# Two transformer blocks on one core: an expert list of 64-byte entries, and the gates' transfers issued by GpSimd in eight pieces

## The chip, the cores and the metric

The kernel is one program on one NeuronCore of a Trainium2 chip. Its engines have their own instruction queues: TensorE (PE; its weight loads are PEld), VectorE (DVE), ScalarE (ACT), GpSimd (POOL) and SyncE (SP). SP, ACT and POOL also issue DMA transfers, which run on 16 DMA engines that the queues share. The metric is the device time of one execution in microseconds (us), lower is better.

## The reference, cut to what matters

Two blocks follow each other on 256 tokens of width 2048. The change lies in the last stage of the second block, a layer that looks up experts. For each token and each of 8 heads it picks 16 of 16,384 experts, and adds up what they give:

```python
sc, ci = lax.top_k(cand, PEER_TOPK)          # cand: sums of two top-16 lists, 256 candidates
idx = e1 * PEER_NKEYS + e2                   # 128 * 128 experts
gate = jax.nn.softmax(sc, axis=-1)
h = jax.nn.gelu(jnp.einsum('cd,chkd->chk', xc, u[ic]))
return jnp.einsum('chk,chkd->cd', gc * h, v[ic])
```

With 256 tokens, 8 heads and 16 picks, most experts are wanted by some token of the 256. The kernel therefore computes `x @ u.T` for all of them, and uses the list of picked experts only for the second product.

## The kernel before, in words

The last stage is the method `peer`. A **group** g (0 to 31) is 512 experts: `fm_group` loads four 1 MB tiles of `in_pu` (SP's queue, L271, three buffers named `raw`), splits each in two halves into a rounded part (ScalarE, L294) and a remainder (VectorE, L295), and multiplies both with the tokens on TensorE (L312 to L314, three matmuls for each product). ScalarE applies GELU (L1526, two rows for each group) into a tile `ge` with two buffers, and GpSimd writes `ge` to rows of the array `R` in device memory (L1528). Each of the four tiles of a group is a **unit**.

Work on the list lies beside the groups. `unit` takes functions from a list `bg` before each load, 1.92 of them for each unit from group 6 on. Those are in order:

- 128 calls of `gates(b, q)`: sixteen of them are a **block** b (0 to 7) of 32 tokens. Each makes one-hot masks on ScalarE (L1412, L1413) and VectorE (L1415), two matmuls (L1417) and an addition into the tile `GB` (two buffers with the tag `gb`). After the sixteenth, the block goes out to `R` and `RD`: L1423 has 15,872 rows of 128 bytes, L1424 has 512 such rows. Both are issued on ScalarE's queue.
- `classes`, `across`, `within`, `places`: each of 15,872 experts gets its place in a list that is sorted by which half of the tokens wants it.
- 31 calls of `scatter` with four indirect transfers each (L1499): each writes 128 expert numbers, 4 bytes each, to their places in `LIST` in device memory.
- `fetch`: when all 124 are complete, the list is read back into `L` (L1506, GpSimd's queue).

After group 31 comes the last part: GpSimd gathers rows of `R` (L1566) and of the experts' values (L1574) by the numbers in `L`, and TensorE multiplies them.

The framework's scheduler fixes the order of each engine's rows before the run. GpSimd's transfers use eight semaphores in turn, so each one also waits until the eighth before it has landed.

Of the kernel before, what the change touches and what calls it, by code (L numbers as in the profile page):

```python
# [11 lines left out]
I32 = mybir.dt.int32  # L12
U32 = mybir.dt.uint32
# [6 lines left out]
P = 128  # L20
T = 256
# [9 lines left out]
EC = 124  # L31
# [96 lines left out]
def prep(i):  # L128
    f = np.float32
    out = {}  # L130
# [5 lines left out]
    o = np.cumsum([0, 256, 256, 512, 512, 16, 1536, 512, 4, 4, 512, 512, 512, 512, 4])  # L136
# [42 lines left out]
    out["pv"] = np.concatenate([pv[:EC].transpose(1, 0, 2).reshape(P * EC, D), pv[EC:].reshape(-1, D)], axis=0)  # L179
    out["ids"] = np.arange(P * EC, dtype=np.int32).reshape(P, EC)  # L180
    out["rel"] = np.concatenate([i["rel_bias_2"], np.ones((1, 32), f)], axis=0)
# [18 lines left out]
class Model:  # L200
# [1149 lines left out]
    def peer(self):  # L1350
# [8 lines left out]
        nc.gpsimd.dma_start(sub, A["subk"].rearrange("p (a n) -> p a n", a=2))  # L1359
        ids = self.t(sp, [P, EC], I32)  # L1360
        nc.gpsimd.dma_start(ids, A["ids"])

        R = self.t(self.dp, [P * EC, 2 * T])
        RD = self.t(self.dp, [P, P - EC, T])
        R3 = R.rearrange("(p e) t -> p e t", p=P)
        LIST = self.t(self.dp, [P * EC, 1], I32)
        E1 = self.t(sp, [P, 2, 8, 16])
# [34 lines left out]
        def gates(b, q):  # L1402
# [19 lines left out]
            if q == 15:  # L1422
                nc.scalar.dma_start(R3[:, :, T + 32 * b:T + 32 * b + 32], GB[0][:, 0:EC])  # L1423
                nc.scalar.dma_start(RD[:, :, 32 * b:32 * b + 32], GB[0][:, EC:P])  # L1424

                dst = F[:, b // 4] if b % 4 == 0 else F4
                nc.vector.tensor_reduce(dst, GB[0], AX.X, ALU.add)
                if b % 4:
                    nc.vector.tensor_add(F[:, b // 4], F[:, b // 4], F4)
# [6 lines left out]
        place, bad = self.t(sp, [P, EC], U32), self.t(ep, [P, 1], I32)  # L1436
        L = self.t(ep, [P, EC], U32)
        got = {}
# [56 lines left out]
        wrote = []  # L1495

        def scatter(lo, hi):
            for e in range(lo, hi):
                i = nc.gpsimd.indirect_dma_start(LIST, bass.IndirectOffsetOnAxis(ap=place[:, e:e + 1], axis=0),  # L1499
                                                 ids[:, e:e + 1], None)  # L1500
                tc.declare_no_dep(i.ins, group="places", reason="the places are different")
                tc.add_to_no_dep_group("places", i.ins)
                wrote.append(i.ins)

        def fetch():
            i = nc.gpsimd.dma_start(L.bitcast(I32), LIST.rearrange("(r c) o -> r (c o)", r=P))  # L1506
            for w in wrote:
                tc.add_manual_dep(i.ins, w.name, mybir.DependencyInfo(mybir.DependencyClass.Sync, mybir.DependencyReason.DATA),
                                  reason="the list is complete")
# [3 lines left out]
        for g in range(32):  # L1513
            if g < 4:
                scores(g)
            if g == 6:
                self.bg.append(turn)
                self.bg += [lambda b=b, q=q: gates(b, q) for b in range(8) for q in range(16)]
                self.bg += [classes, lambda: None, across, lambda: None, within, places]
                self.bg += [lambda e=e: scatter(e, e + 4) for e in range(0, EC, 4)]  # L1520
                self.bg += [fetch]
                self.rate = 1.92
# [39 lines left out]
        def gather(pool, cs):  # L1562

            rt = self.t(pool, [P, 4, 2 * T], tag="rt")
            for e, c in enumerate(cs):
                nc.gpsimd.indirect_dma_start(rt[:, e], None, R, bass.IndirectOffsetOnAxis(ap=L[:, c:c + 1], axis=0))  # L1566
            n = len(cs)
# [5 lines left out]
        def listed(c, r):  # L1573
            nc.gpsimd.indirect_dma_start(r, None, A["pv"], bass.IndirectOffsetOnAxis(ap=L[:, c:c + 1], axis=0))  # L1574
            return r
# [145 lines left out]
```

## Time and profile before

| what | value |
|---|---|
| median of 3 runs | 3310.65 us (3301.16 to 3317.48) |
| the profiled execution's own time | 3312.3 us |
| its span, first to last instruction | 3310.5 us |
| TensorE busy | 2990.0 us (90%) |
| VectorE, ScalarE, GpSimd busy | 2154.5, 1558.8, 498.5 us |
| mean granted TensorE clock | 0.952 of full |
| groups 0 to 31 of the last stage | 1754 to 2804 us of the span |

The profile is of one execution. Issuing a transfer doesn't count as busy time on ScalarE and SP. A busy TensorE says little by itself, so what ends its idle time is read from the waits and from rows in order of time.

### The profile page before, as it was taken

Reading aid. Unit: us, or ns where it says so; the run is one execution under the profiler, and the core shown is the slowest. Engines: PE = TensorE matmul, PEld = TensorE weight load, DVE = VectorE, ACT = ScalarE, POOL = GpSimd, SP = SyncE. Lnnn points to the kernel's source line nnn. Section 1 sums busy time; section 2 is a strip of 40 time slices with the busy share of each in tenths; the row PEclk is TensorE's granted clock in tenths of the full one; section 3 lists DMA queues with packets and bytes.
Section 4 is the critical chain, followed back from the end, with each engine's and each line's share of the span. In section 5 each row is a group of like instructions: output and inputs, shape, how many; then the busy total and the mean of one; then the engine's idle time right before and its main releaser. Section 6 shows DMA issues by size and latency. Waiting matters only on the chain.

```text
span 3310.5 us, 53445 instructions
## 1 busy us (share of the span) xinstructions
PE 2990.0 (90%) x21356; PEld 2781.8 (84%) x21356; DVE 2154.5 (65%) x3842; ACT 1558.8 (47%) x2604; POOL 498.5 (15%) x468
## 2 busy tenths in 40 slices
PE   5989988999999999999999998788883599999998
PEld 4678878999999999887899998788783589777776
DVE  7678987786555555745669977677770134666665
ACT  1163443544444344557554466566550133555545
POOL 3100000000000000200000000000007521556552
PEclk9999999999999999989999999899986799999999
DMA  9955677685655555433345556666661246788886
GB/s 403 386 208 191 216 265 250 218 324 198 245 194 186 183 187 184 163 141 112 129 164 181 183 204 187 177 196 193 181 192 53 96 173 222 263 290 282 299 283 214
DMA packets 253043, 696.66 MB, mean 210 GB/s; under 512 B 149226, under 2 KB 149290, under 8 KB 190832
## 3 DMA queue, kind: packets, MB, share of 16 engines
q1 hardware_dynamic: 75600, 472.29, 40.2%
q0 software_dynamic: 44816, 199.83, 16.8%
q10 hardware_dynamic: 132368, 21.03, 3.6%
q8 instruction: 170, 2.79, 0.3%
q14 instruction: 89, 0.73, 0.1%
HBM read 657.58 MB, written 41.53 MB: 211 GB/s over the span
## 4 chain that ended last, share of the span: by engine, by line
PE 60%; DMA 9%; DVE 8%; issue 7%; ACT 5%; POOL 4%; ACTq 4%; another core or an unknown queue 1%; DVEq 0%; SPq 0%; POOLq 0%
PE t L314 18%; PE t L312 18%; PE t L313 18%; DMA t<-in_wmod 4%; DMA t<-in_pv,t 4%; ACTq L1424 3%; DVE t L295 3%; POOL t L1566 2%; ACT t L294 1%; PE t L310 1%; DVE t L421 1%; PE t L1229 1%; POOL t L1574 1%; ACT t L1260 1%
## 5 line engine op out<-in xcount | busy, mean ns | idle before, releaser
L312 PE MATMUL t<-t,t 128*128 128x256 f32 (+2 forms) x6376 | 1912.8, 301 | 128.6 <-ACT t L294 48.2
L314 PE MATMUL t<-t,t 128*128 128x256 f32 (+2 forms) x6376 | 1905.7, 300 | 42.9 <-DVE t L295 23.8
L313 PE MATMUL t<-t,t 128*128 128x256 f32 (+2 forms) x6376 | 1909.5, 300 | 36.3 <-issue 19.4
L295 DVE TENSOR_TENSOR t<-t,t 128x1024 fp32r<-128x1024 f32 (+2 forms) x938 | 1135.2, 1217 | 808.4 <-ACT t L294 730.0
L294 ACT ACTIVATE t<-t 128x1024 fp32r<-128x1024 f32 (+2 forms) x938 | 982.0, 1052 | 1182.0 <-PE t L313 694.3
L312 PEld LDWEIGHTS t<-t,t 128*128 128x128 f32 x6376 | 1239.3, 194 | 178.6 <-ACT t L294 56.5
L313 PEld LDWEIGHTS t<-t,t 128*128 128x128 f32 x6376 | 1239.8, 194 | 81.4 <-issue 25.7
L314 PEld LDWEIGHTS t<-t,t 128*128 128x128 f32 x6376 | 1237.3, 195 | 83.9 <-DVE t L295 30.2
L421 DVE CUSTOM_DVE_ANT_0 t<-t,t,t 128x1024 f32<-128x1024 f32 x192 | 244.7, 1279 | 59.0 <-DMA t<-in_wmod 58.7
L1415 DVE TENSOR_SCALAR t<-t,t,t 128x128 fp32r<-128x128 f32 x512 | 142.8, 341 | 39.2 <-PE t L1417 39.1
L1574 POOL DMA_INDIRECT t<-in_pv,t x103 | 140.3, 1362 | 179.2 <-DVE t L295 148.1
L1528 POOL DMA_DIRECT2D t<-t x31 | 23.6, 761 | 875.5 <-ACT t L1526 418.5
L1566 POOL DMA_INDIRECT t<-t,t x103 | 137.9, 1339 | 50.7 <-issue 26.8
L1499 POOL DMA_INDIRECT t<-t,t x124 | 126.2, 1018 | 48.0 <-issue 37.5
L310 PE MATMUL t<-t,t 128*128 128x256 f32 (+1 forms) x448 | 116.2, 422 | 13.2 <-ACT t L523 7.1
L310 PEld LDWEIGHTS t<-t,t 128*128 128x128 f32 x448 | 87.5, 197 | 41.8 <-issue 19.7
L1420 ACT ACTIVATE t<-t 128x256 f32<-128x256 f32 x128 | 44.6, 399 | 107.3 <-issue 104.2
L1412 ACT ACTIVATE t<-t,t 128x128 f32<-128x128 f32 x256 | 89.3, 397 | 0.1
L1421 DVE TENSOR_TENSOR t<-t,t 128x256 f32<-128x256 f32 x128 | 49.0, 420 | 60.3 <-ACT t L1420 60.2
L1102 POOL DMA_DIRECT2D t<-in_w2c x1 | 0.6, 564 | 455.3 <-DMA t<-in_win 455.3
L1072 POOL DMA_DIRECT2D t<-in_oh x1 | 0.6, 566 | 454.4 <-PE t L389 454.4
L1417 PE MATMUL t<-t,t 128*128 128x256 f32 x256 | 45.9, 292 | 24.9 <-ACT t L1413 24.8
(393 smaller groups left out, 1821.3 us busy)
## 6 DMA issues: line engine op xcount, KB each, us to landing
t<-in_pu SPq DMA_DIRECT2D x128, 1024.0 KB, 4.8
t<-in_win SPq DMA_DIRECT2D x64, 1024.0 KB, 5.9
t<-in_wmod SPq DMA_DIRECT2D x122, 512.0 KB, 5.9
t<-in_wg SPq DMA_DIRECT2D x44, 1024.0 KB, 4.8
t<-in_wu SPq DMA_DIRECT2D x44, 1024.0 KB, 4.8
t<-in_wd SPq DMA_DIRECT2D x44, 1024.0 KB, 5.0
t<-in_wmod POOLq DMA_DIRECT2D x70, 512.0 KB
t<-in_wout SPq DMA_DIRECT2D x32, 1024.0 KB, 5.4
```

Source lines behind the costliest of these rows:

```text
L294: nc.scalar.activation(h[:, :w], r[:, o:o + w], AF.Copy)
L295: nc.vector.tensor_sub(l[:, :w], r[:, o:o + w], h[:, :w].bitcast(F32))
L310: mm(ps, wh, xh, start=start, stop=stop, skip_group_check=True)
L312: mm(ps, wh, xh, start=start, stop=False, skip_group_check=True)
L313: mm(ps, wh, xl, start=False, stop=False, skip_group_check=True)
L314: mm(ps, wl, xh, start=False, stop=stop, skip_group_check=True)
L421: nc.vector.tensor_tensor_reduce(r, r, self.cb[:, s], 1.0, init, ALU.mult, ALU.add, dst)
L1415: nc.vector.tensor_scalar(o1[:, k], iota, ET[:, 0, t:t + 1], GH[:, k, t:t + 1].bitcast(F32), ALU.is_equal, ALU.mult)
L1424: nc.scalar.dma_start(RD[:, :, 32 * b:32 * b + 32], GB[0][:, EC:P])
L1499: i = nc.gpsimd.indirect_dma_start(LIST, bass.IndirectOffsetOnAxis(ap=place[:, e:e + 1], axis=0), ids[:, e:e + 1], None)
L1566: nc.gpsimd.indirect_dma_start(rt[:, e], None, R, bass.IndirectOffsetOnAxis(ap=L[:, c:c + 1], axis=0))
L1574: nc.gpsimd.indirect_dma_start(r, None, A["pv"], bass.IndirectOffsetOnAxis(ap=L[:, c:c + 1], axis=0))
```

## The change

Part one is the list. An entry of `LIST` grows from one number of 4 bytes to 16 copies of it, 64 bytes; the input `ids` holds each number 16 times, and each scatter writes 128 entries of 64 bytes. `ids` (1 MB in place of 62 KB) is loaded late, by the new `numbers`, into a buffer of the tag `gb`. The fetch (1 MB in place of 62 KB) moves from GpSimd's queue to SP's, and the gathers read every sixteenth number of `L16`. Part two is the gates: the transfer to `R` is issued by GpSimd in eight pieces of 16 partitions (1,984 rows of 128 bytes each), and the one to `RD` by GpSimd behind them.

```diff
@@ -177,7 +177,7 @@
 
     pv = i["peer_v_2"][0].reshape(P, P, D)
     out["pv"] = np.concatenate([pv[:EC].transpose(1, 0, 2).reshape(P * EC, D), pv[EC:].reshape(-1, D)], axis=0)
-    out["ids"] = np.arange(P * EC, dtype=np.int32).reshape(P, EC)
+    out["ids"] = np.repeat(np.arange(P * EC, dtype=np.int32), 16).reshape(P, EC * 16)
     out["rel"] = np.concatenate([i["rel_bias_2"], np.ones((1, 32), f)], axis=0)
     pos = np.concatenate([np.concatenate([i[n][0].T] * 2, axis=0) for n in ("cmp_pos_k_2", "cmp_pos_v_2")], axis=1)
     v = {
@@ -1357,13 +1357,11 @@
         XH, XL = self.XH, self.XL
         sub = self.t(sp, [P, 2, P])
         nc.gpsimd.dma_start(sub, A["subk"].rearrange("p (a n) -> p a n", a=2))
-        ids = self.t(sp, [P, EC], I32)
-        nc.gpsimd.dma_start(ids, A["ids"])
 
         R = self.t(self.dp, [P * EC, 2 * T])
         RD = self.t(self.dp, [P, P - EC, T])
         R3 = R.rearrange("(p e) t -> p e t", p=P)
-        LIST = self.t(self.dp, [P * EC, 1], I32)
+        LIST = self.t(self.dp, [P * EC, 16], I32)
         E1 = self.t(sp, [P, 2, 8, 16])
         E2 = self.t(sp, [P, 2, 8, 16])
         GG = self.t(sp, [P, 2, 8, 16])
@@ -1420,8 +1418,9 @@
             nc.scalar.activation(gb, pv[:, 1], AF.Copy)
             nc.vector.tensor_add(gb, pv[:, 0], gb)
             if q == 15:
-                nc.scalar.dma_start(R3[:, :, T + 32 * b:T + 32 * b + 32], GB[0][:, 0:EC])
-                nc.scalar.dma_start(RD[:, :, 32 * b:32 * b + 32], GB[0][:, EC:P])
+                for p in range(0, P, 16):
+                    nc.gpsimd.dma_start(R3[p:p + 16, :, T + 32 * b:T + 32 * b + 32], GB[0][p:p + 16, 0:EC])
+                nc.gpsimd.dma_start(RD[:, :, 32 * b:32 * b + 32], GB[0][:, EC:P])
 
                 dst = F[:, b // 4] if b % 4 == 0 else F4
                 nc.vector.tensor_reduce(dst, GB[0], AX.X, ALU.add)
@@ -1434,7 +1433,7 @@
         MT, BT = self.t(sp, [EC, 4, P]), self.t(sp, [P, 8])
         PO, PI, PF = self.t(sp, [P, EC]), self.t(sp, [P, 2, EC], I32), self.t(sp, [P, 2, EC])
         place, bad = self.t(sp, [P, EC], U32), self.t(ep, [P, 1], I32)
-        L = self.t(ep, [P, EC], U32)
+        L16 = self.t(ep, [P, EC * 16], U32)
         got = {}
 
         def classes():
@@ -1494,16 +1493,21 @@
 
         wrote = []
 
+        def numbers():
+            got["ids"] = self.t(sp, [P, EC * 16], I32, tag="gb", bufs=2)
+            nc.gpsimd.dma_start(got["ids"], A["ids"])
+
         def scatter(lo, hi):
+            ids = got["ids"]
             for e in range(lo, hi):
                 i = nc.gpsimd.indirect_dma_start(LIST, bass.IndirectOffsetOnAxis(ap=place[:, e:e + 1], axis=0),
-                                                 ids[:, e:e + 1], None)
+                                                 ids[:, 16 * e:16 * e + 16], None)
                 tc.declare_no_dep(i.ins, group="places", reason="the places are different")
                 tc.add_to_no_dep_group("places", i.ins)
                 wrote.append(i.ins)
 
         def fetch():
-            i = nc.gpsimd.dma_start(L.bitcast(I32), LIST.rearrange("(r c) o -> r (c o)", r=P))
+            i = nc.sync.dma_start(L16.bitcast(I32), LIST.rearrange("(r c) o -> r (c o)", r=P))
             for w in wrote:
                 tc.add_manual_dep(i.ins, w.name, mybir.DependencyInfo(mybir.DependencyClass.Sync, mybir.DependencyReason.DATA),
                                   reason="the list is complete")
@@ -1516,7 +1520,7 @@
             if g == 6:
                 self.bg.append(turn)
                 self.bg += [lambda b=b, q=q: gates(b, q) for b in range(8) for q in range(16)]
-                self.bg += [classes, lambda: None, across, lambda: None, within, places]
+                self.bg += [classes, numbers, across, lambda: None, within, places]
                 self.bg += [lambda e=e: scatter(e, e + 4) for e in range(0, EC, 4)]
                 self.bg += [fetch]
                 self.rate = 1.92
@@ -1563,7 +1567,7 @@
 
             rt = self.t(pool, [P, 4, 2 * T], tag="rt")
             for e, c in enumerate(cs):
-                nc.gpsimd.indirect_dma_start(rt[:, e], None, R, bass.IndirectOffsetOnAxis(ap=L[:, c:c + 1], axis=0))
+                nc.gpsimd.indirect_dma_start(rt[:, e], None, R, bass.IndirectOffsetOnAxis(ap=L16[:, 16 * c:16 * c + 1], axis=0))
             n = len(cs)
             WH, WL = weighted(pool)
             nc.vector.tensor_mul(rt[:, :n, 0:T], rt[:, :n, 0:T], rt[:, :n, T:2 * T])
@@ -1571,7 +1575,7 @@
             return WH, WL
 
         def listed(c, r):
-            nc.gpsimd.indirect_dma_start(r, None, A["pv"], bass.IndirectOffsetOnAxis(ap=L[:, c:c + 1], axis=0))
+            nc.gpsimd.indirect_dma_start(r, None, A["pv"], bass.IndirectOffsetOnAxis(ap=L16[:, 16 * c:16 * c + 1], axis=0))
             return r
```

On ScalarE the end of block 1, before the change (`t_20938` is this block's `GB`):

```order
L1412 ACTIVATE t_21745<-t_74,t_16977 128x128
L1412 ACTIVATE t_21753<-t_74,t_16977 128x128
L1423 DMA t_16971<-t_20938 15872x1x32
L1424 DMA t_16972<-t_20938 512x1x32
L1420 ACTIVATE t_21723<-t_21724 128x128x2
L1413 ACTIVATE t_21744<-t_21745 128x128
L1413 ACTIVATE t_21752<-t_21753 128x128
L294 ACTIVATE t_21768<-t_21762 128x1024
L1420 ACTIVATE t_21723<-t_21743 128x128x2
```

The same place after the change (`t_20943` is this block's `GB`; lines are two lower):

```order
L1418 ACTIVATE t_20943<-t_21628 128x128x2
L1418 ACTIVATE t_20943<-t_21647 128x128x2
L1411 ACTIVATE t_21737<-t_21738 128x128
L1411 ACTIVATE t_21745<-t_21746 128x128
L1410 ACTIVATE t_21757<-t_74,t_16975 128x128
L1410 ACTIVATE t_21765<-t_74,t_16975 128x128
L1411 ACTIVATE t_21756<-t_21757 128x128
L1411 ACTIVATE t_21764<-t_21765 128x128
L294 ACTIVATE t_21780<-t_21774 128x1024
```

The two transfers are gone from ScalarE; the next block's masks follow at once on the block's last copies.

On GpSimd, from the write of group 22 to the fetch, before the change (`t_16971` is `R`, `t_16973` is `LIST`, and "x25" is 25 such rows in a run):

```order
L1528 DMA t_16971<-t_26613 128x4x256
L1499 DMA t_16973<-t_16969,t_16989 15872x1 x25
L1528 DMA t_16971<-t_26902 128x4x256
L1499 DMA t_16973<-t_16969,t_16989 15872x1 x43
L1528 DMA t_16971<-t_27172 128x4x256
L1499 DMA t_16973<-t_16969,t_16989 15872x1 x42
L1528 DMA t_16971<-t_27442 128x4x256
L1499 DMA t_16973<-t_16969,t_16989 15872x1 x14
L1506 DMA t_16991<-t_16973 128x124
L1528 DMA t_16971<-t_27708 128x4x256
```

On GpSimd after the change, from the pieces of block 7 to the last scatter (`t_16969` is `R`, `t_16970` is `RD`, `t_16971` is `LIST`, `t_26609` is `ids`; L1532 writes groups 22 to 26 in this order):

```order
L1422 DMA t_16969<-t_25810 1984x1x32 x8
L1423 DMA t_16970<-t_25810 512x1x32
L1498 DMA t_26609<-in_ids 128x1984
L1532 DMA t_16969<-t_26669 128x4x256
L1532 DMA t_16969<-t_26958 128x4x256
L1503 DMA t_16971<-t_26609,t_16987 15872x16 x44
L1532 DMA t_16969<-t_27228 128x4x256
L1503 DMA t_16971<-t_26609,t_16987 15872x16 x32
L1532 DMA t_16969<-t_27498 128x4x256
L1503 DMA t_16971<-t_26609,t_16987 15872x16 x28
L1532 DMA t_16969<-t_27764 128x4x256
L1503 DMA t_16971<-t_26609,t_16987 15872x16 x20
```

The gates' nine transfers and the load of `ids` now stand ahead of the write of group 22, the writes of groups 22 and 23 ahead of the first scatter, and the writes of groups 24, 25 and 26 behind 44, 76 and 104 scatters (before, 23, 24 and 25 behind 25, 68 and 110). The fetch has left this queue.

On SP after the change, around the fetch (L1510):

```order
L271 DMA t_28145<-in_pu 128x2048
L271 DMA t_28203<-in_pu 128x2048
L1510 DMA t_16989<-t_16971 128x1984
L271 DMA t_28267<-in_pu 128x2048
L271 DMA t_28325<-in_pu 128x2048
```

The row of the fetch is new here. The two loads above it are the last of group 28. Below it stand the twelve of groups 29 to 31, of which two are shown.

## Rows read from the trace of the kernel before

**Rows 1.** The page: the span, and two lines of the 40 equal slices (82.8 us each): TensorE's busy tenths and the tenths of full clock that it was granted; then the issues of the groups' loads (count, KB each, median us from issue to landing).
```profile
span 3310.5 us, 53445 instructions
PE   5989988999999999999999998788883599999998
PEclk9999999999999999989999999899986799999999
...
t<-in_pu SPq DMA_DIRECT2D x128, 1024.0 KB, 4.8
```

**Rows 2.** Lines L1423 and L1424 alone (`ACTq` is ScalarE's queue; shortest, median and longest in ns, first and last start in us). The landing time is that of L1423, from issue to the last byte.
```profile
L1423 ACTq DMA_DIRECT2D t<-t x8: 520/521/596, 2003.1 to 2447.5; - x8
DMA to landing us min/median/max: 16.7/16.7/16.7
...
L1424 ACTq DMA_DIRECT2D t<-t x8: 13702/13966/14959, 2003.7 to 2448.1; - x8
```

**Rows 3.** ScalarE in order of time (start us, us): the second of the two GELU rows of groups 7, 8, 9 and 22.
```profile
2001.19 0.58 ACT L1526 ACTIVATE t<-t 128x512 f32<-128x512 f32 x1
2038.73 0.58 ACT L1526 ACTIVATE t<-t 128x512 f32<-128x512 f32 x1
2063.55 0.58 ACT L1526 ACTIVATE t<-t 128x512 f32<-128x512 f32 x1
2468.87 0.60 ACT L1526 ACTIVATE t<-t 128x512 f32<-128x512 f32 x1 [0.46 <-PE t L314]
```

**Rows 4.** Busy time in three stretches, whose columns are: length, busy us of PE, PEld, DVE, ACT, POOL (instructions in brackets), granted clock, busy share of the 16 DMA engines, GB/s. The first stretch is the first gate block before its transfers, the second a hold of ScalarE's queue at L1424, the third the block after it.
```profile
1950.00:2003.00 53.00, 52.89 (x443) 52.72 (x442) 44.82 (x106) 43.31 (x116) 2.26 (x3) 1.00 0.54 192
2323.50:2337.50 14.00, 7.14 (x58) 6.72 (x56) 7.22 (x10) 0.00 (x0) 0.00 (x0) 0.92 1.00 172
2337.50:2385.50 48.00, 46.67 (x363) 46.26 (x364) 39.12 (x87) 38.47 (x100) 1.51 (x2) 0.92 0.56 194
```

**Rows 5.** DMA queues from 2448 to 2466 us, which holds one block's transfers: packets, MB, share of the 16 engines (q10 is ScalarE's queue, q1 SP's).
```profile
q10 hardware_dynamic: 16416, 2.10, 74.3%
q1 hardware_dynamic: 34, 0.16, 5.3%
```

**Rows 6.** What a plain DMA costs GpSimd: L419 (128 rows of 4 KB, 537 ns in the mean, from the groups by line), L1528 (512 rows of 1 KB, shortest, median, longest), the two L1082 in order of time (2048 rows of 1536 bytes each; in square brackets the idle time before and what ended it), and the landing of the last L1528 out of the chain of work (start us, us).
```profile
L419 POOL DMA_DIRECT2D t<-in_wmod x70 | 37.4, 537 | 88.0 <-DMA t<-in_wmod 52.6 <-DVE t L421 15.8 <-DVE t L541 6.1
L1528 POOL DMA_DIRECT2D t<-t x31: 754/754/806, 1757.0 to 2778.5; - x31
874.67 1.04 POOL L1082 DMA_DIRECT2D t<-t  x1 [2.53 <-DMA t<-t]
895.66 1.03 POOL L1082 DMA_DIRECT2D t<-t  x1 [19.45 <-DMA t<-t]
2778.53 3.66 DMA t<-t
```

**Rows 7.** GpSimd: the scatters as a whole, then rows in order of time from the first scatter to the fetch (square brackets: the idle time before, and what ended it).
```profile
L1499 POOL DMA_INDIRECT t<-t,t x124: 967/971/1883, 2482.0 to 2675.2; - x124
2481.96 1.07 POOL L1499 DMA_INDIRECT t<-t,t  x1 [10.54 <-DVE t L1484]
2515.50 0.81 POOL L1528 DMA_DIRECT2D t<-t  x1
2570.54 0.97 POOL L1499 DMA_INDIRECT t<-t,t  x1 [0.30 <-issue]
2593.13 0.81 POOL L1528 DMA_DIRECT2D t<-t  x1 [21.62 <-ACT t L1526]
2678.04 0.58 POOL L1506 DMA_DIRECT2D t<-t  x1 [1.85 <-DMA t<-t,t]
```

**Rows 8.** ScalarE in order of time: the last GELU row of groups 23, 29, 30 and 31.
```profile
2501.82 0.58 ACT L1526 ACTIVATE t<-t 128x512 f32<-128x512 f32 x1
2754.61 0.58 ACT L1526 ACTIVATE t<-t 128x512 f32<-128x512 f32 x1
2777.65 0.58 ACT L1526 ACTIVATE t<-t 128x512 f32<-128x512 f32 x1
2803.72 0.58 ACT L1526 ACTIVATE t<-t 128x512 f32<-128x512 f32 x1
```

**Rows 9.** Busy time in stretches within and after the scatters, columns as in rows 4.
```profile
2520.00:2540.00 20.00, 5.37 (x15) 3.94 (x14) 0.00 (x0) 1.06 (x1) 15.13 (x17) 0.50 0.05 11
2540.00:2560.00 20.00, 2.90 (x8) 2.02 (x7) 1.23 (x1) 0.00 (x0) 15.43 (x16) 0.50 0.02 0
2580.00:2600.00 20.00, 20.00 (x165) 20.00 (x165) 9.31 (x8) 8.02 (x10) 5.65 (x5) 0.97 0.63 225
2680.00:2780.00 100.00, 99.65 (x819) 99.66 (x820) 43.01 (x36) 41.69 (x45) 3.81 (x5) 0.98 0.60 217
```

**Rows 10.** TensorE in order of time inside the scatters ("issue" is a wait that no profiled event ends), and what all DMA queues moved from 2500 to 2580 us, in 40 slices of 2 us.
```profile
2556.04 0.37 PE L312 MATMUL t<-t,t 128*128 128x256 f32 x1 [2.43 <-issue]
2558.84 0.37 PE L313 MATMUL t<-t,t 128*128 128x256 f32 x1 [2.43 <-issue]
GB/s 71 8 1 0 1 0 1 37 303 346 101 1 1 0 1 0 1 0 1 1 0 0 1 1 0 1 0 1 0 1 0 0 1 0 1 0 0 0 0 0
```

**Rows 11.** GpSimd's 103 gathers of R rows (busy us, mean ns), and the stretch in which the gathers run, columns as in rows 4.
```profile
L1566 POOL DMA_INDIRECT t<-t,t x103 | 137.9, 1339 | 50.7 <-issue 26.8 <-DVE t L383 15.9 <-PE t L314 4.0
2800.00:3250.00 450.00, 432.79 (x1847) 342.02 (x1848) 290.17 (x244) 227.52 (x222) 257.76 (x191) 0.99 0.80 281
```

## The prediction

> **What bounds the kernel now.** I read the slices of the page first. TensorE is busy in nine tenths of nearly every slice, so the kernel goes at TensorE's pace except where something starves it. Two places stand out in the last stage [rows 1]: from slice 24 to 29 its busy tenths and its clock are a little down, and in slices 30 and 31 (2483 to 2648 us) they are 3 and 5, with the clock at 6 and 7 tenths.
>
> The first place is the gate blocks. The queue rows of ScalarE show that L1423 issues in 0.52 us, but L1424 behind it holds the queue for 13.97 us in the median, eight times [rows 2]. ScalarE makes the rounded halves of every weight tile, so TensorE soon has nothing: in one hold it is busy for 7.14 us of 14, and afterwards it runs for a while at the lower of its two clocks (0.92 is the mean of the stretch that follows). A block without a hold has 52.89 of 53 us at clock 1.00 [rows 4]. The GELU rows give the price: groups 7 to 22 take 467.7 us, 31.2 each, while two neighbours with no hold between them (8 and 9) are 24.82 us apart [rows 3]. Fifteen such groups would be 372.3 us. The eight holds cost 95.4 us, 11.9 each.
>
> The second place is the scatters. They are issued every 1.27 us (0.97 plus an idle 0.30) from 2482 us on, and TensorE falls from 20 busy us in 20 to 5.37 and 2.90, at clock 0.50 [rows 7, 9]. The waits name no event: single matmuls stand 2.8 us apart, after an idle time put down to "issue", and all DMA queues together move almost nothing in this stretch, not even SP's loads [rows 10]. When GpSimd stops at 2571.5 us, because its next transfer waits 21.62 us for a late GELU, the loads flow again and TensorE is busy in all 20 us from 2580 to 2600 [rows 7, 9]. So the scatters starve loads and TensorE's instructions alike. Indirect transfers as such don't: in the last part the gathers issue in 1.34 us each, and TensorE is busy in 432.79 of 450 us with DMA at 281 GB/s [rows 11]. What differs is the tiny write. Groups 23 to 31 end 334.9 us after group 22 [rows 3, 8]; at the undisturbed 23.04 us [rows 8], with 26.07 for the last, they would take about 210.
>
> **The change, part by part.** *Gates off ScalarE.* Its queue loses 8 x 14.5 us, and the loads' rounding follows at once. What is next is TensorE's own pace of 24.8 us a group: in an unheld block VectorE is busy for 44.82 and ScalarE for 43.31 of 53 us [rows 4], so neither takes over. Gain 95 us; the bounds are 55 (only the 6.9 idle us of each hold) and 112 (each hold whole).
>
> *Gates on GpSimd.* No row shows 1,984 rows of 128 bytes there. From below, L1082 with 2,048 longer rows takes 1.04 us; from above, L419 at 537 ns for 128 rows is 4.2 ns a row, or 8.3 us a piece [rows 6]. I take the slope from L419 to L1528, 217 ns for 384 more rows: 0.57 ns a row, 1.6 us a piece, since L1082 shows that the price per row falls with the number. A block is then eight pieces, L1423 and two writes, about 15 us of GpSimd in 52, which idles there. The landing: in its present queue a block occupies 74.3% of 18 us, 13.4 us of all engines [rows 5]; beside the 0.54 of 53 us that an unheld block uses [rows 4] that makes 42 of 52 us. From above, the 3 MB of an L1082 landed within 20 us, 9.8 ns a row, or 160 us for 16,384 rows [rows 6]; but that moves 1,536 bytes a row, and by bytes it is 14. I take 13 to 25 us, within what `GB`'s two buffers allow. Three `raw` buffers cover about 17 us of slow loads. Cost 0; if the cover goes, see the rivals.
>
> *Entries of 64 bytes.* The lower bound is the starvation of 4-byte writes, the upper one the 128-byte rows of the gates, which run at 157 GB/s (2.10 MB in 13.4 us) with no trickle [rows 5]. 64 is half of 128 and sixteen times 4, so I take the latter: the scatters no longer starve anyone. Their issue stays at 1.27 us, the same 128 entries each.
> The Trainium skill ("DMA: Bandwidth & Descriptors", Specifications) speaks against this: transfers under 512 bytes are done by read-modify-write, and 64 is far under. By it the stall would stay, the second rival below. The trace disagrees for 128 bytes and says nothing of 64.
>
> *What then sets the scatters' stretch* is GpSimd's queue. I count from the second GELU of group 23. Its write goes at 1.4 us, then 44 scatters (56 us), write 24 at 57.5, landed at 61 (3.66 us [rows 6]); 32 scatters, write 25 landed at 103; 28, write 26 landed at 139; 20, all issued at 162, and the fetch's wait over at 163.5 (1.85 us after the last, as now [rows 7]). `ge` has two buffers, so the GELU of 26 needs write 24 (due 69, free at 61), that of 27 needs write 25 (due 92, free at 103), that of 28 write 26 (due 126, free at 139). The loads of group 29 stand behind the fetch on SP: issued at 163.5, landed 4.8 us later [rows 1], rounded by 169.4. Groups 29, 30 and 31 then end at 192, 215 and 241.5 (the last 26.07). Now it is 301.9 [rows 8]: 60 us gained. Group 23, which takes 32.95 us now [rows 3, 8], comes before the first scatter in the new order and takes 24: 9 more.
>
> *The rest costs nothing.* `ids` is 1 MB behind block 7's pieces, some 5 us of landing after 15 us of issue, and is wanted at the first scatter, some 33 us after block 7's end. The fetch of 1 MB lands in about 5 us and is wanted after group 30's write, some 45 us later. The gathers read the same 128 numbers, 64 bytes apart.
>
> Sum against the profiled execution's 3312.3 us (the runs' median is 3310.65, so no correction): 3312.3 - 95 - 69 = **3148 us**.
>
> **Rivals.** *1. The entries still starve (the change doesn't do what it says).* For: 64 bytes are small, and no row shows that size. Against: the 128-byte rows. The scatters then take 196 us as now [rows 7] from group 23 on, with 24 to 26 done inside, and five groups follow: 292 to 315 us, against 301.9 now. With group 23's 9 us that is a gain of about 10, and 3312 - 95 - 10 = 3207.
>
> *2. The holds move to the loads.* The blocks' rows still occupy all 16 engines for 13.4 us, and during a hold q1 moved only 0.16 MB [rows 5]. For: if SP's loads get no share, TensorE starves as before. Against: in a hold nothing asked for loads, as ScalarE freed no buffer, and the cover is 17 us. With no gain there: 3312 - 69 = 3243.
>
> *3. Slower: GpSimd's pieces set the pace.* At 8.3 us a piece, a block takes 69 us of GpSimd against 63.5 now (444.4 us between the first and last L1423, over 7 [rows 2]): 8 x 5.5 = 44 lost. Block 7's pieces then end some 37 us after group 23, and the scatters start late by that: 69 - 37 = 32 gained. That is 3324, and each microsecond more a piece adds 72 (64, and 8 of delay); the change is slower from about 8.2 us a piece on, or a landing as late as that. Against: L1528's 31 are 754 to 806 ns, in blocks with VectorE at 85% as after them [rows 4, 6].
> The Trainium skill ("SBUF — State Buffer", the section on the two separate sides) has GpSimd locked out of writing descriptors while VectorE runs certain instructions, 620 ns becoming 3100. By this ratio a piece of 1.6 us would take 8, and the time would be about 3300. The trace disagrees: L1528 doesn't stretch.
>
> **How the numbers follow.** The forecast has 0.58, rival 1 has 0.2, rival 2 0.1, rival 3 0.08, and 0.04 is left for losses and gains that cancel. The predicted time is the first one's, 3148. Its own range is 3131 to 3188, from the bounds of the holds (112 and 55). The range for all reaches upward over rival 1 with its spread of 23 us and stops short of rival 2, and downward by the 13 us of the wait for GELU 28, should GpSimd's chain run ahead of my count: 3118 to 3235, some 0.8. A measurement of this kernel can tell 0.5%, 16 us: faster 0.88 (forecast, rivals 1 and 2), same 0.04, slower 0.08.
>
> **What would show it.** Right: no row of ScalarE's queue over 1 us in the blocks, groups 7 to 22 at 25 us each, pieces under 3 us; TensorE busy from the first scatter on at clock 1.00, no matmuls 2.8 us apart; a wait of about 12 us before the GELUs of 27 and 28, and one of some 30 us for the loads behind the fetch. Wrong: pieces of 7 us or more, or writes of `ge` that land over 45 us late; TensorE waiting for loads inside the blocks; DMA at zero while scatters run; scatters over 1.8 us apart, since then GpSimd's chain eats the 60 us.

## The result, and the profile after

The changed kernel takes 3216.7 us (median of 4 runs, 3201.2 to 3224.2) against 3314.1 (4 runs, 3301.2 to 3325.9): a ratio of 0.970, 95% interval 0.965 to 0.975. The profiled execution took 3216.31 us, 96 less than that of before; 164 were forecast.

Line numbers have moved: the gates' transfers are L1422 and L1423, the scatters L1503, the fetch L1510, the GELUs L1530, the writes of `ge` L1532. The page, as in [rows 1]: the two dips of the last stage are now one, in slice 31, with TensorE at 3 tenths and its clock at 5.

```profile
span 3214.5 us, 53638 instructions
PE   5989978999999999999999999999998389999998
PEclk9999999999999999999999999999999599999999
```

GpSimd's lines for the gates, which took the place of [rows 2] (shortest, median, longest in ns):

```profile
L1422 POOL DMA_DIRECT2D t<-t x64: 1007/1032/1080, 2002.9 to 2395.2; - x64
...
L1423 POOL DMA_DIRECT2D t<-t x8: 774/782/827, 2011.0 to 2396.2; - x8
```

A piece costs 1.03 us, a block 8 x 1.03 + 0.78 = 9 us of GpSimd. No hold is left on ScalarE's queue.

ScalarE in order of time, second GELU rows of groups 7, 8, 9, then 22 (a row of two, the second begins some 0.5 us later), 23 and 31, as in [rows 3, 8]:

```profile
2000.71 0.58 ACT L1530 ACTIVATE t<-t 128x512 f32<-128x512 f32 x1
2028.01 0.58 ACT L1530 ACTIVATE t<-t 128x512 f32<-128x512 f32 x1
2050.22 0.58 ACT L1530 ACTIVATE t<-t 128x512 f32<-128x512 f32 x1
...
2399.32 1.08 ACT L1530 ACTIVATE t<-t 128x512 f32<-128x512 f32 x2
2427.72 0.58 ACT L1530 ACTIVATE t<-t 128x512 f32<-128x512 f32 x1
...
2711.59 0.58 ACT L1530 ACTIVATE t<-t 128x512 f32<-128x512 f32 x1
```

Groups 7 to 22 take 399.1 us in place of 467.7: 68.6 gained. Groups 23 to 31 end 311.8 us behind group 22, in place of 334.9: 23.1 gained. With 0.5 us ahead of group 7 and 3.9 behind group 31 that is the whole 96.

What is left in the gates' stretch: busy time from 2000 to 2400 us, columns as in [rows 4], before and then after.

```profile
2000.00:2400.00 400.00, 338.27 (x2673) 334.01 (x2671) 289.77 (x606) 238.55 (x612) 9.80 (x13) 0.91 0.66 188
...
2000.00:2400.00 400.00, 384.38 (x3128) 378.73 (x3127) 339.32 (x704) 279.89 (x709) 83.09 (x88) 0.99 0.78 215
```

TensorE went from 338 to 384 busy us of 400, its mean clock from 0.91 to 0.99, and GpSimd from 10 to 83. But the groups alternate: group 8, beside a block's transfers, took 27.3 us and group 9 22.2, and the next pair 33.9 and 21.9. The list of waits from 1960 to 2425 us (total us, times, longest) names what is new:

```profile
ACT t L294 <- DMA t<-in_pu: 34.4, 9, 6.4
```

Nine waits of ScalarE for late loads; the same list of the kernel before has none. TensorE's own waits in it come to 15.4 us (63.6 before). The DMA engines' share rose from 0.66 to 0.78. The queues from 2002 to 2024 us, which begin with the first block's transfers (columns as in [rows 5]; q0 is GpSimd's queue), show who shares them: the 16 engines are full for the whole 22 us, and the loads of q1 get a third of them.

```profile
q0 software_dynamic: 681, 2.25, 64.0%
q1 hardware_dynamic: 413, 3.00, 35.5%
```

The scatters in the changed kernel, and TensorE beside them (columns as in [rows 4]; answers to [rows 7, 9]):

```profile
L1503 POOL DMA_INDIRECT t<-t,t x124: 963/967/2015, 2429.7 to 2616.1; - x124
...
2440.00:2460.00 20.00, 20.00 (x169) 20.00 (x168) 6.72 (x6) 7.28 (x8) 15.91 (x14) 1.00 0.45 157
2540.00:2560.00 20.00, 3.73 (x10) 2.59 (x9) 0.00 (x0) 0.00 (x0) 15.12 (x17) 0.50 0.03 7
2580.00:2600.00 20.00, 20.00 (x154) 20.00 (x154) 8.58 (x7) 8.16 (x9) 9.96 (x9) 0.90 0.49 169
```

They start 52 us earlier than before, and some 30 us pass undisturbed, but the starvation comes all the same: 3.73 busy us of 20, clock 0.50, 7 GB/s. It leaves when GpSimd pauses (2574 to 2588 us, for a late GELU). Its matmuls are those of [rows 10], one of which:

```profile
2559.22 0.37 PE L313 MATMUL t<-t,t 128*128 128x256 f32 x1 [2.43 <-issue]
```

Behind them stands something that the forecast had not seen. ScalarE in order of time, after the GELU of group 27 (2609.76 us):

```profile
2618.28 0.36 ACTq L1544 DMA_DIRECT2D t<-in_fin  x1
2618.74 2.96 ACT L294 ACTIVATE t<-t 128x1024 fp32r<-128x1024 f32 x3 [8.39 <-remote]
```

L1544 loads the weights of the last norm for the stage that follows. Its line stands behind the whole loop, but in ScalarE's order it is ahead of the loads' rounding for group 28, and as its tile takes memory of the stage that the scatters still read, the program has it wait for all of GpSimd's scatters. Whatever ScalarE does next waits with it: 8.39 us here, as the groups are late themselves.

### The profile page after: what moved, and what is told of

The parts are those of the page before. It is cut to its first block, busy times and chain, and to the rows that moved or that the text cites. A ratio compares the mean times of both kernels' runs of the same rounds, so it can differ in the third digit from the quotient of the medians.

```text
span 3214.5 us, 53638 instructions
## 1 busy us (share of the span) xinstructions
PE 2972.2 (92%) x21356; PEld 2765.2 (86%) x21356; DVE 2154.8 (67%) x3842; ACT 1558.9 (48%) x2604; POOL 569.0 (18%) x539
## 5 line engine op out<-in xcount | busy, mean ns | idle before, releaser
L1578 POOL DMA_INDIRECT t<-in_pv,t x103 | 133.8, 1299 | 183.2 <-DVE t L295 150.9
L1503 POOL DMA_INDIRECT t<-t,t x124 | 134.0, 1081 | 37.8 <-issue 37.8
L1532 POOL DMA_DIRECT2D t<-t x31 | 23.9, 772 | 654.9 <-ACT t L1530 348.4
L1422 POOL DMA_DIRECT2D t<-t x64 | 64.8, 1033 | 59.2 <-DVE t L1419 33.9
L1411 ACT ACTIVATE t<-t 128x128 fp32r<-128x128 f32 x256 | 65.6, 306 | 7.6 <-PE t L1415 7.6
L383 DVE TENSOR_TENSOR t<-t,t 128x1024 fp32r<-128x1024 f32 (+3 forms) x62 | 61.4, 1012 | 2.6 <-ACT t L382 2.6
```

## Experiments

The first four ran on a chip on which the kernel before takes 3282.5 us (3274.1 to 3294.6, 13 runs), the others on three chips where it takes 3311 to 3315 us, close to the 3314 of the result. Ratios are to the kernel before on the same chip.

### The two parts apart

The list alone: the gates' lines as in the kernel before.

```
-                for p in range(0, P, 16):
-                    nc.gpsimd.dma_start(R3[p:p + 16, ...], GB[0][p:p + 16, 0:EC])
-                nc.gpsimd.dma_start(RD[...], GB[0][:, EC:P])
+                nc.scalar.dma_start(R3[...], GB[0][:, 0:EC])
+                nc.scalar.dma_start(RD[...], GB[0][:, EC:P])
```

> The list alone: 64 bytes an entry, the numbers loaded late, the list fetched by SyncE; the gates' transfers stay on ScalarE's queue. If the two parts add up, this is worth what the stretch from GELU 22 to GELU 31 lost between the traces, 335 to 312 us: about 3290 us, TensorE starved again from some 45 us after the first scatter. If the forecast's term for the scatters (69 us) was right and something in the gates' part took it back, it is about 3245 us.

Measured: 3280.7 us, ratio 0.999 (0.998 to 1.001). The list part is worth nothing there. And, against the first branch, nothing starved in the way of [rows 10], yet the second branch's 3245 didn't come either. ScalarE in order of time, SyncE's wait at the fetch, and TensorE's busy time ahead of the stop and in it:

```profile
2652.27 0.35 ACTq L1543 DMA_DIRECT2D t<-in_fin  x1
2652.72 2.95 ACT L294 ACTIVATE t<-t 128x1024 fp32r<-128x1024 f32 x3 [99.58 <-DMA t<-t,t]
...
SPq L1509 <- DMA t<-t,t: 100.1, 3, 97.7
...
2540.00:2550.00 10.00, 10.00 (x86) 10.00 (x85) 3.68 (x4) 5.02 (x6) 7.87 (x8) 1.00 0.61 215
2570.00:2580.00 10.00, 0.00 (x0) 0.00 (x0) 0.00 (x0) 0.00 (x0) 7.87 (x9) 0.50 0.08 25
```

TensorE runs at full pace beside some 70 us of scatters of 64 bytes 1.3 us apart, then stops outright for 94 us, while ScalarE stands at the norm's weights (L1543 here) and SyncE at the fetch, both until the last scatter.

The gates alone: the kernel before with the gates' lines of the change.

> The gates' transfers on GpSimd alone; the list keeps 4 bytes an entry and is fetched by GpSimd. If the parts add up: groups 7 to 22 at 399 us in place of 468, so about 3245 us, with the starving from the first 10 us on as in the kernel before. If the starving is set by what GpSimd still has on its way from the gates when the scatters begin, its onset moves too and the gain from GELU 22 to GELU 31 is not 0.

Measured: 3173.5 us, ratio 0.968 (0.963 to 0.972). The changed kernel itself was not run on this chip, but the gates alone win there what the whole change wins in the result (0.970), and the list alone won nothing. ScalarE's rows (a GELU of group 27, the norm's weights, the next roundings), then the scatters as a whole, with 4-byte entries, and the last GELU rows of groups 23 and 31:

```profile
2523.34 0.60 ACT L1527 ACTIVATE t<-t 128x512 f32<-128x512 f32 x1 [9.42 <-DMA t<-t]
...
2583.76 0.34 ACTq L1541 DMA_DIRECT2D t<-in_fin  x1
2584.19 2.95 ACT L294 ACTIVATE t<-t 128x1024 fp32r<-128x1024 f32 x3 [58.82 <-DMA t<-t,t]
```

```profile
L1500 POOL DMA_INDIRECT t<-t,t x124: 963/967/1880, 2403.7 to 2581.5; - x124
...
2424.55 0.58 ACT L1527 ACTIVATE t<-t 128x512 f32<-128x512 f32 x1
...
2675.06 0.58 ACT L1527 ACTIVATE t<-t 128x512 f32<-128x512 f32 x1
```

Again no matmuls 2 us apart: the wait of 9.42 us before GELU 27 is the one forecast at 12, GELU 31 is 250.5 us behind GELU 23 where 241.5 was forecast for the changed kernel, and 58.8 us go to ScalarE's wait. On this chip the 4-byte list starves nothing, which the forecast expected of 64 bytes only.

### Without scatters, and with reads

No scatters: the calls are left out, and the list is loaded from the table of numbers.

```
-                i = nc.gpsimd.indirect_dma_start(LIST, ..., ids[:, 16 * e:16 * e + 16], None)
+                pass
-            i = nc.sync.dma_start(L16.bitcast(I32), LIST.rearrange(...))
+            nc.sync.dma_start(L16.bitcast(I32), A["ids"])
```

> The changed kernel without its scatters: the list is filled with the plain numbers in order, so the rows that the last phase gathers are others, as many and as large. If the scatters alone starve TensorE, the nine groups from GELU 22 to GELU 31 take about 23 us each as groups 28 to 30 do after the changed kernel's list is complete, 210 us in place of 312: about 3115 us. If the instruction supply fails there for another reason (the parts of the program laid far apart, the throttle), the matmuls stand 2 us apart again and the time is within 20 us of 3217.

Measured: 3114.5 us, ratio 0.948 (0.944 to 0.952). GELU 22 (second of the row) to GELU 31:

```profile
2391.25 1.08 ACT L1523 ACTIVATE t<-t 128x512 f32<-128x512 f32 x2
...
2608.10 0.58 ACT L1523 ACTIVATE t<-t 128x512 f32<-128x512 f32 x1
```

216 us, as expected. The scatters, by whatever way, cost some 60 us there beside the gates alone.

Reads in place of writes: the same transfers, by the same places, from the table of numbers into on-chip memory. The list is loaded from the table as without scatters, so SyncE's fetch waits for none of them, and the scheduler lays the write of group 23 behind 12 of them, not ahead of all.

```
-                i = nc.gpsimd.indirect_dma_start(LIST, IndirectOffsetOnAxis(place...), ids[...], None)
+                nc.gpsimd.indirect_dma_start(to[:, 16 * e:16 * e + 16], None, table, IndirectOffsetOnAxis(place...))
```

> The changed kernel with each scatter turned round: the same 124 indirect transfers of 128 entries of 64 bytes, by the same places, read from device memory into on-chip memory; the list is then the plain numbers in order, as without scatters. Theory A, that small writes to device memory are what starves: TensorE stays busy, GpSimd's queue still paces the groups through the writes that stand behind the transfers, about 3150 to 3180 us. Theory B, that a row of indirect transfers 1.3 us apart starves the others whatever their direction: matmuls 2 us apart from about 45 us on, about 3217 us.

Measured: 3176.0 us, ratio 0.967 (0.963 to 0.971). All the reads, and TensorE beside them:

```profile
L1504 POOL DMA_INDIRECT t<-in_ids,t x124: 947/952/1972, 2415.0 to 2585.8; - x124
...
2480.00:2500.00 20.00, 20.00 (x169) 20.00 (x168) 8.42 (x8) 8.50 (x9) 15.43 (x16) 1.00 0.62 222
```

No slow matmuls. But since the writes of the two runs before made none on this chip either, it doesn't tell theory A from B. It was repeated elsewhere, below.

### The same kernels on another chip, and the norm's weights moved

> The kernel before once more, with a trace of its own on the chip of these runs. In the four runs so far no matmuls stood 2 us apart; TensorE stopped outright while ScalarE's queue stood at the transfer of the last norm's weights (L1543 in the run with the list alone), which waits until GpSimd's scatters are all done, 99.6 us there. Theory C, that this wait sets the time and the matmuls 2 us apart are a side matter that comes in some executions and not in others: about 3280 us, last scatter about 2650 us, GELU 31 some 129 us behind the last scatter, as in both traces with the gates on ScalarE (2803.7 - 2675.2 and 2779.0 - 2650.0). Theory D, that the slow matmuls belong to the 4-byte list when it follows the gates on ScalarE: matmuls 2 us apart again and a last scatter near 2675 us.

Measured: 3316.2 us (one run). All the scatters, and TensorE's waits from 2425 to 2620 us (total us, times, longest):

```profile
L1499 POOL DMA_INDIRECT t<-t,t x124: 963/967/2003, 2481.2 to 2671.7; - x124
...
PE t L312 <- issue: 24.5, 13, 7.5
```

The slow matmuls are back. Theory C doesn't hold here.

> The changed kernel once more beside the others. Theory C: without the slow matmuls the last scatter comes at about 2585 us, as with the gates alone (2581.5) or with reads (2585.8), and GELU 31 some 94 us later: about 3176 us, a ratio near 0.968. Theory D, that 64-byte writes behind the gates' transfers on one queue starve TensorE: about 0.98 of the kernel before and matmuls 2 us apart.

Measured: 3219.2 us, ratio 0.971 (0.968 to 0.973), last scatter at 2616.7 us, 35 later than the gates alone on the first chip. In the same list of waits:

```profile
L1503 POOL DMA_INDIRECT t<-t,t x124: 963/967/2018, 2423.9 to 2616.7; - x124
...
PE t L312 <- issue: 28.1, 20, 2.4
```

Then the gates alone once more, with the norm's weights on GpSimd's queue; and the changed kernel with the same line:

```
-        nc.scalar.dma_start(w, A["fin2"].to_broadcast([P, D]))
+        nc.gpsimd.dma_start(w, A["fin2"].to_broadcast([P, D]))
```

> The gates alone, and the weights of the last norm loaded by GpSimd in place of ScalarE, so that ScalarE's queue no longer stands until the scatters are done. Theory C: TensorE's stop of 52 us ahead of group 28 goes; the groups then wait only for their gated units' writes, which stand between scatters on GpSimd's queue (the write of group 27 at 2582.5 us lands some 4 us later, then GELU 29): GELU 31 at about 2635 us in place of 2675, so about 3133 us, a ratio near 0.955. If GpSimd's indirect transfers themselves hold up loads and instructions, the stop stays and the time is within 10 us of 3173.

Measured: 3218.0 us, ratio 0.971 (0.969 to 0.974), neither of the two times expected: the slow matmuls came here too. The scatters, and TensorE's wait:

```profile
L1500 POOL DMA_INDIRECT t<-t,t x124: 963/967/2028, 2398.4 to 2607.8; - x124
...
PE t L312 <- issue: 19.9, 16, 2.4
```

> The changed kernel whole, with the weights of the last norm loaded by GpSimd in place of ScalarE. SyncE's queue still stands at the list's fetch until the scatters are done, with the loads of groups 28 on behind it. Theory C with a second hold: the wait moves from ScalarE's transfer to the loads and nothing is won, within 10 us of the changed kernel. If ScalarE's transfer was the only hold that counted: about 40 us below the changed kernel.

Measured: 3222.4 us, ratio 0.973 (0.969 to 0.976).

The last three can't be told apart. The last two differ in the list alone, and groups 23 to 31 end 311.3 us behind group 22 in both (311.8 in the result's trace). Where the slow matmuls come, neither the list (its entry's size, and the queue of its fetch) nor the place of the norm's weights matters: the starved groups are late, GpSimd's queue stands for their writes between scatters, and the last scatter comes at 2608 to 2617 us in place of 2582. Whether moving the norm's weights helps where no matmul is slow was not tried.

### What in the scatters starves

The reads once more, now where the kernel before takes 3310.7 us:

> The scatters turned round into reads once more (the list is the plain numbers in order, so other rows are gathered, as many and as large). The earlier run of it was on a chip where the kernel before takes 3282 us; there neither reads nor writes made matmuls stand 2 us apart. On a chip where the kernel before takes 3314 us its own scatters do so. Where that is so again, theory A (small writes to device memory starve the engines): TensorE busy until it stops for ScalarE's transfer, last read about 2586 us, about 3176 us, a ratio near 0.958. Theory B (a close row of indirect transfers starves them, whatever their direction): matmuls 2 us apart from some 20 to 50 us behind the first read on, about 3217 us, 0.971.

Measured: 3210.0 us, ratio 0.969 (0.965 to 0.974). All reads, TensorE's busy time, and one of its rows:

```profile
L1504 POOL DMA_INDIRECT t<-in_ids,t x124: 947/952/2006, 2415.2 to 2602.9; - x124
...
2500.00:2520.00 20.00, 3.93 (x10) 2.88 (x10) 0.00 (x0) 0.00 (x0) 15.18 (x16) 0.50 0.08 7
...
2519.26 0.37 PE L312 MATMUL t<-t,t 128*128 128x256 f32 x1 [2.42 <-issue]
```

Reads starve as writes do. Theory A is out as the one cause; and the kernel that ran free on the first chip starves on this one, so the chip (or the occasion) decides as well.

Plain writes: as many entries of 64 bytes, each column written to 128 neighbouring places.

```
-                i = nc.gpsimd.indirect_dma_start(LIST, IndirectOffsetOnAxis(place...), ids[:, 16 * e:16 * e + 16], None)
+                i = nc.gpsimd.dma_start(LIST[P * e:P * e + P], ids[:, 16 * e:16 * e + 16])
```

> The changed kernel with each scatter replaced by a plain transfer of GpSimd: the same 128 entries of 64 bytes, written in a row of the list in place of scattered (the list then holds the numbers in another order, so other rows are gathered, as many and as large). Where the kernel before takes 3314 us: theory A (many small writes, however addressed) has matmuls 2 us apart again and about 3217 us; theory B (only the indirect form, in which GpSimd reads the places and makes each address, starves) has TensorE busy until ScalarE's transfer stops it, at GpSimd's pace of about 1.1 to 1.3 us an entry column: 3150 to 3180 us.

Measured: 3117.3 us, ratio 0.941 (0.937 to 0.946). All the writes, and TensorE beside them:

```profile
L1503 POOL DMA_DIRECT2D t<-t x124: 538/538/553, 2428.5 to 2513.0; - x124
...
2480.00:2500.00 20.00, 20.00 (x169) 20.00 (x169) 8.42 (x8) 8.49 (x9) 15.24 (x29) 1.00 0.64 224
```

Twice as dense (124 in 84.5 us, 0.68 us each), as small, to the same tensor: and TensorE is busy in all 20 us of this stretch and of each of the nine others from 2400 to 2600. On the DMA queue they look like the reads that starve: below, GpSimd's queue in 10 us with 16 plain writes, then in 20 us with 16 of the reads above (2440 to 2450 and 2500 to 2520; packets, MB, share).

```profile
q0 software_dynamic: 544, 0.14, 6.6%
q0 software_dynamic: 512, 0.13, 7.9%
```

These small writes starve nobody. They differ from the scatters in two things, though: they are plain, and their places are neighbours. No run has plain transfers to scattered places, or indirect ones to neighbouring places, so which of the two counts is not shown. The time is lower than I had expected even under theory B, as the plain form costs GpSimd 0.54 us in place of 0.97 and leaves its queue free by 2514 us. It builds no usable list, so it is a bound and no version.

Paused scatters: a multiplication on GpSimd ahead of each.

```
+                p = nc.gpsimd.tensor_mul(pad, pad, pad)    # 128x400, ordered ahead of the scatter
                 i = nc.gpsimd.indirect_dma_start(LIST, ..., ids[:, 16 * e:16 * e + 16], None)
```

> The changed kernel with a multiplication of 128x400 numbers on GpSimd ahead of each scatter, by the row of 128x1024 (3.34 us) about 1.3 us: the scatters start some 2.6 us apart in place of 1.3, 124 of them over about 325 us. GELU 31 then waits for the last scatter plus about 94 us: last scatter near 2755 us, about 3350 us. The question is how TensorE runs meanwhile: theory E, that starving needs scatters faster than something behind them takes them, has no matmuls 2 us apart at half the pace, only stops for the writes that stand behind scatters and for ScalarE's transfer. If it is each scatter that hurts and not their pace, the slow matmuls fill the whole stretch of 325 us, and the time goes above 3400 us through the later writes.

Measured: 3284.5 us, ratio 0.990 (0.986 to 0.994). All scatters (2.4 us apart in the mean, 2.7 in the first 60 us, in which TensorE runs), TensorE at full pace and then stopped, the GELU row that ends the stop, and one of VectorE's subtractions:

```profile
L1509 POOL DMA_INDIRECT t<-t,t x124: 998/1009/1952, 2431.7 to 2725.1; - x124
...
2480.00:2500.00 20.00, 19.35 (x162) 19.15 (x160) 14.56 (x7) 6.35 (x6) 18.67 (x15) 1.00 0.51 168
2500.00:2520.00 20.00, 0.00 (x0) 0.00 (x0) 0.00 (x0) 0.00 (x0) 18.14 (x20) 0.58 0.15 53
...
2542.35 0.60 ACT L1538 ACTIVATE t<-t 128x512 f32<-128x512 f32 x1 [45.61 <-DMA t<-t]
...
2470.84 2.27 DVE L295 TENSOR_TENSOR t<-t,t 128x1024 fp32r<-128x1024 f32 x1 [0.59 <-ACT t L294]
```

No slow matmuls in 293 us of scatters (no wait of TensorE there is put down to "issue"): it runs, or it stands for a write of `ge` that waits between scatters (45.6 us here, 161.2 in four such waits). So pace matters, as far as this run can say: the same indirect writes 2.4 us apart don't starve here, 1.3 us apart they do in the result's trace. The time falls short of the 3350 expected in two parts: the pause took 0.87 us, not 1.3, so the last scatter came 30 us earlier, and GELU 31 followed it after 56 us, not 94. The pause is no clean tool, though: VectorE's subtraction takes 2.27 us beside it, 1.22 in the mean without.

A version from these findings: gates on GpSimd, 4-byte list, norm's weights on GpSimd, a pause of 128x160 ahead of each scatter, and

```
-                nc.gpsimd.dma_start(R3[:, 4 * g:4 * g + 4, 0:T], ge)
+                nc.scalar.dma_start(R3[:, 4 * g:4 * g + 4, 0:T], ge)
```

> A version built from the findings: the gates on GpSimd; the list with 4 bytes an entry and fetched by GpSimd; the weights of the last norm loaded by GpSimd, so that ScalarE's queue stands nowhere for the scatters; the gated units' writes issued by ScalarE behind their own GELU, so that none stands between scatters; and a multiplication of 128x160 on GpSimd ahead of each scatter (about 0.55 us), which makes them some 1.7 us apart, between the 1.3 us at which matmuls stood 2 us apart and the 2.4 us of the paused run, where none did. If 1.7 us is slow enough: no slow matmuls and no stop, 23 us a group from group 23 on, GELU 31 near 2610 us as without scatters, last scatter near 2620 us, about 3120 us, a ratio of 0.942. If 1.7 us is still too fast: matmuls 2 us apart from some tens of us behind the first scatter until the last, near 2620 us, five to seven groups of 23 us still to come: 3210 us or more.

Measured: 3400.7 us, ratio 1.026 (1.022 to 1.029): slower than the kernel before. All scatters, and TensorE beside and behind the last groups:

```profile
L1506 POOL DMA_INDIRECT t<-t,t x124: 999/1007/2040, 2672.6 to 2885.9; - x124
...
2680.00:2700.00 20.00, 20.00 (x169) 20.00 (x168) 10.38 (x9) 8.49 (x9) 18.35 (x18) 1.00 0.70 211
2720.00:2740.00 20.00, 0.00 (x0) 0.00 (x0) 0.00 (x0) 0.00 (x0) 17.76 (x25) 0.50 0.01 0
```

The first scatter comes at 2672.6 us in place of 2404. With the writes on ScalarE the scheduler laid the gate units in other places: the gates' transfers end at 2652 us, so the scatters run after the groups and TensorE stands idle beside them. The order of instructions would have told this before the run. Groups 30 and 31 ran beside scatters 1.73 us apart without slow matmuls, but that is only 35 us, and the starvation took 10 to 45 us to set in elsewhere. Whether that pace is slow enough stays open.

## Why the prediction came out as it did

The sign and the range (3118 to 3235) held; the sum, 3148, missed by 68 us. The likeliest case didn't come. Rival 1 did: the entries still starve. That the time lies within 10 us of its price of 3207 is partly luck: it takes 95 us for the gates, where 68.6 came, and 10 for the list, where 23.1 came, and the two misses partly cancel.

*Gates off ScalarE: right in kind, mis-sized.* 95 us were forecast (55 to 112), 68.6 came. All eight holds went, TensorE's pace took over, but at 26.6 us a group and not 24.8. The missing 27 us are more than a quarter of rival 2, which I had put at nothing or all. Some 16 of them are idle time of TensorE (384.38 busy us of 400), and some 11, by an estimate, are slower work: by the row with clock 1.00 in [rows 4], 443 matmuls in 52.89 us, its 3128 matmuls would take 373.5. "Cost 0", with 17 us of `raw` buffers as cover, was the step that failed: beside the first block's rows the loads get a third of the DMA engines for 22 us, longer than the cover, and over the eight blocks ScalarE waits 34.4 us for loads. That these waits cause the idle time is followed link by link at the longest only: ScalarE's 6.39 us, which end at 2135.86, are followed by 2.72 us in which TensorE waits for the rounding. The size of the term itself is steady: in the ten traces with this order of the gates on GpSimd groups 7 to 22 take 392 to 400 us, in the three with them on ScalarE 468.

*Gates on GpSimd: right.* A piece took 1.03 us (1.6 taken, bounds 1.04 to 8.3), by L1082, the lower bound, and not by the slope. Rival 3 had nothing for it: all 64 pieces lie between 1.007 and 1.080 us with VectorE busy in 85% of the stretch. So the lock-out that the Trainium skill describes ("SBUF — State Buffer", the section on the two separate sides) shows in none of them; whether VectorE ran an instruction of the kind that the page means is not shown.

*Entries of 64 bytes: wrong.* 69 us were forecast, 23.1 came: 5.0 in group 23 in place of 9, and 18.0 behind it in place of 60. "What differs is the tiny write" was the failed step. The 128-byte rows and the scatters differ in size, but also in form (plain or indirect), and the gathers, which I took to clear the indirect form, differ from the scatters in pace: GpSimd's 191 rows in 450 us [rows 11] are one in 2.4 us, and the scatters come every 1.27; closer than 1.8 us the gathers come for 9 us at most, less than the 10 us or more after which the stall set in. Size was not the difference: on one chip the list with 4 bytes (fetched by GpSimd) and with 64 (fetched by SyncE) gave 0.971 and 0.973, both with slow matmuls. What is left is the form, or the scattered places that came with it (plain writes to neighbours don't starve, indirect reads do), and the pace (paused scatters don't starve). The 23 us came without larger entries: the gates on GpSimd with 4 bytes gave the same 311.3 us behind group 22, against 338.7 in the trace of the kernel before on that chip.
The rule on transfers under 512 bytes in the Trainium skill ("DMA: Bandwidth & Descriptors", Specifications) led the prediction to the right outcome, that the stall would stay (rival 1, which it calls the second there), but not by the right cause: plain writes of 64-byte entries ran without harm, and reads, which write nothing to device memory, starved.

*GpSimd's chain: about right in length where nothing starves, but it ended at the wrong hold.* The changed kernel was never traced without the stall, so the nearest is the gates alone on the first chip, with the write of group 23 behind 12 of the scatters and the fetch on GpSimd's queue: the last scatter started 157.0 us behind GELU 23, with 162 forecast, and GELU 31 came after 250.5, with 241.5 forecast. I had the loads behind the fetch as the last wait; ScalarE's transfer for the next stage waits for the same scatters, with the roundings of group 28 on behind it. I didn't look for transfers of later stages that the scheduler had moved forward.

## What to carry to other kernels

Before a cure is built on the one thing in which a harmful transfer differs from a harmless one, write down all in which they differ (size, form, places, direction, pace): one run for each is cheap, and here size, the most natural guess, was not it. Look in each queue's order for a transfer of the next stage that waits for memory of this one; here it stopped all that stood behind it on ScalarE, for 99.6 us in the longest case. And an experiment on a stall should run where the stall is: the first four runs here were on a chip that didn't show it.

## What the runs showed that I had not expected

Indirect transfers of GpSimd 1.3 us apart brought TensorE to a matmul every 2 to 3 us and all loads to a trickle in the seven traces of three occasions (the result's two, those of the second four experiments, and the reads repeated), from 10 to 45 us behind the first one on, in either direction and at 4 and 64 bytes. On one chip three such kernels ran free, and the kernel before is 1% faster there (3282.5 against 3311 to 3315). That the kernel before runs free there is inferred from its time; it has no trace of that chip. What passes between GpSimd and the other engines' instructions in that state no trace shows: the DMA engines are busy for 0.02 to 0.08 of it in the rows shown. It stays open, and so does what sets the chips apart.

A plain transfer of 128 entries costs GpSimd 0.54 us (the plain writes), an indirect one 0.97 and some 0.3 ahead of the next (the scatters of the changed kernel).

A multiplication of 128x400 on GpSimd (0.87 us) stretched VectorE's subtraction of two 128x1024 tiles from 1.22 to between 2.1 and 2.5 us. The Trainium skill ("SBUF — State Buffer", the section on the two separate sides) has VectorE and GpSimd share a pair of ports that one of them holds for a whole instruction; these rows agree, as 1.22 and 0.87 make 2.09.
